# Two of four depthwise-convolution blocks moved from VectorE to ScalarE and GpSimd

## The chip, the cores and the metric

The kernel runs on one core of a Trainium2 chip. A core has a matrix engine (TensorE, PE in the rows), a vector engine (VectorE, DVE), an engine for activation functions (ScalarE, ACT), a general engine (GpSimd, POOL) and a queue that issues transfers (SyncE, SP). Each of them works through its own instructions in order, and they wait for each other on semaphores. On-chip data lies in SBUF (128 partitions); PE writes to PSUM.

The metric is the device time of one execution in microseconds (us), lower is better.

## The reference

A trunk of two layers on 512 tokens of 1024 channels, in float32. Each layer mixes tokens in three parallel branches, merges them with gates, and adds a feed-forward block and a gated per-layer input:

```python
proj = h @ w_in[i]
qa, ka, va, glu_in, qc, kc, vc, gates = jnp.split(proj, SPLITS, axis=-1)
ya = diff_attention(qa, ka, va, ...)
yb = conformer_conv(glu_in, conv_w[i], conv_b[i], cln_g[i], cln_b[i])
yc = neighbourhood_attention(qc, kc, vc, rpb[i])
ga, gb, gc = jnp.split(jax.nn.sigmoid(gates), 3, axis=-1)
merged = (ga * (ya @ w_br_a[i]) + gb * (yb @ w_br_b[i])
          + gc * (yc @ w_br_c[i]))
x = x + merged @ w_o[i]
```

The change is in the convolution of branch b: 512 channels, each with 31 taps of its own along the tokens, then a bias, a layer norm over the channels and a SiLU:

```python
a, g = jnp.split(u, 2, axis=-1)
z = a * jax.nn.sigmoid(g)
z = lax.conv_general_dilated(z, conv_w, window_strides=(1,), padding=[(15, 15)],
                             feature_group_count=CB, ...)
z = layernorm(z + conv_b, cln_g, cln_b)
return jax.nn.silu(z)
```

## The kernel before

Activations lie transposed: channels on the partitions, the 512 tokens along the free dimension, so that 512 channels are four blocks of 128x512. Every product with weights is made of three matmuls (`mm3`, L179): weights and activations are each split into a high part (a rounded copy, made by ScalarE) and a low part (the remainder, a subtraction on VectorE), both stored as float32r. `weights` (L170) loads a weight tile into a `wr` buffer, makes `wh` on ScalarE and `wl` on VectorE; there are three buffers of each, so the split of a tile waits until PE has done with the tile three before it. A tile is 128x1024 for a projection of the layer's input (24 matmuls of 512 columns, below called p), and 128x512 for a branch's output weights (12 matmuls, below called b).

PE's order is the order in which the code is written. The other engines' instructions are ordered by a scheduler from priorities (the place in the code, with pulls forward for weights) and from when it takes their inputs to be ready; on the chip each engine then keeps that order and waits where an input is late.

The order of a layer's phases: the gated input of the convolution (glu), neighbourhood attention (natten), differential attention (diff) with the gates of branch c (gatec) between, then branch c (`branch_c`, L786: one b tile for each of eight column blocks m), two of the gates of b (gateb, m = 2 and 3), merge a (`merge_a`, L793: for each of eight blocks a p tile for the gate and then a b tile), then `conv` (L566: sums the four convolution blocks, layer norm, SiLU), the remaining gates of b, merge b, the output projection, the feed-forward block.

The convolution itself is a list of VectorE instructions: for each of the four blocks j (`glu_z` tiles in, `conv_z` tiles out) one `tensor_scalar` with the bias and then 30 `scalar_tensor_tensor` (`c = src * w + c`), 124 in a layer. `taps` (L539) yields them one after another, and `background` (L554) takes a few at each of many places in the phases, as many as the table `BG` (L49) says, each placed behind a named instruction of its phase. By the sums of the table, 56 are issued up to the first two gates of b, and the rest in branch c, gates of b and merge a; `conv` issues what is left over.

The tiles that matter: `conv_z` and `glu_z` share five `z` buffers, so the third output block must wait until the taps of the second block have read their input; `rp` has four buffers, and is used by the query and key rotation of diff, by the split of the convolution's sum, and later in the output projection.

Of the kernel before, what the change touches and what calls it, by code (L numbers as in the profile page):

```python
# [14 lines left out]
AF = mybir.ActivationFunctionType  # L15
ALU = mybir.AluOpType
# [4 lines left out]
P = 128  # L21
# [3 lines left out]
GR = 8  # L25
# [5 lines left out]
CON3W = 31  # L31
# [15 lines left out]
PAR = L * PAR_L + 8  # L47
WARM = 8
BG = dict(glu=2, natten=1, values=3, diff=1, gatec=2, branchc=2, gateb=4, mergea=4, mergea2=2)  # L49
FIRST = (["v"] * 4 + ["pt"] * 2 + ["y", "b"], ["y"] * 5 + ["pt"] * 2 + ["b"])  # L50
EARLY = 6
QUARTERS = (2, 4, 6)
# [13 lines left out]
class Net:  # L66
# [229 lines left out]
    def build(self):  # L296
        nc, tc, a = self.nc, self.tc, self.a
        self.bufs = dict(wr=3, wh=3, wl=3, h=8, qk=2, kh=2, v=4, pt=2, y=5, z=5, x=4, t=7, rp=4,
                         e=4, a=3, r=2, rb=1, ss=1, sm=8, rc=4, b=2, s=8)
        self.bg, self.w_ahead = BG, 400  # L300
        self.pbufs = dict(mm=3, sc=2, tr=2, av=1)
# [12 lines left out]
    def opening(self):  # L314
# [23 lines left out]
        for k in range(KD):  # L338
# [6 lines left out]
            if k == 0:  # L345
                first = head[:, KD:]
                nc.vector.tensor_copy(hi[:, :P], first)
                self.tt(lo[:, :P], first, hi[:, :P].bitcast(F32), ALU.subtract)
            h.append(self.operand(xc[k], head[:, k:k + 1], FIRST[0][k]))
            c = slice(0 if k else P, 512)  # L350
# [81 lines left out]
    def layer(self, i, h, xsrc, xs):  # L432
        self.i, self.h = i, h
        zs, cs = [], []
        self.todo = self.taps(zs, cs)
        self.glu(zs)
        if i == 0:
            self.lambdas()
        yc, ya, yb = [], [], []
        sn, sd = {}, {}  # L440
        self.natten_in(0, sn, yc)
        self.drain(self.renorm)
        self.h = self.hs
        self.natten_v(sn)
        last = self.glu_last(zs)
        self.natten_in(1, sn, yc)
        next(last)
        self.natten_in(2, sn, yc)
        next(last)
        self.natten_in(3, sn, yc)  # L450
        acc, gb = [], []
        self.diff_in(0, sd, ya)
        self.diff_v(0, sd)
        self.diff_in(1, sd, ya)
        self.gate_c(acc, 0)
        self.diff_in(2, sd, ya)
        self.diff_v(1, sd)
        self.diff_in(3, sd, ya)
        for m in range(1, KD):
            self.gate_c(acc, m)  # L460
        for m in range(2):
            self.gate_b(gb, m, AF.Copy, None)
        for g in acc + gb:
            self.act(g, g, AF.Sigmoid, table="sigmoid")
        self.branch_c(acc, yc)
        for m in range(2, 4):
            self.gate_b(gb, m, AF.Sigmoid, "sigmoid")
        self.merge_a(ya, acc)
        conv = self.run(self.conv(cs, yb))
        pairs = self.inputs()  # L470
        for m in range(4, KD):
            self.gate_b(gb, m, AF.Sigmoid, "sigmoid")
            for n in ((0, 1), (2,), (3,), ())[m - 4]:
                self.input_block(pairs, n)
        self.drain(conv)
        mg = self.merge_b(yb, acc, gb)
        ws = self.pair_weights(4)
        x, h = self.w_o(mg, xsrc)
        self.input_pair(ws, pairs, 4)
        h = self.ffn(h, x)  # L480
        return self.ple(h, x, xs, self.inputs())
# [56 lines left out]

    def taps(self, zs, cs):  # L539

        for j, z in enumerate(zs):
            zf = z.rearrange("p a b -> p (a b)")
            c = self.sb("z", [P, 512])
            cs.append(c)
            for d in range(CON3W):
                w = self.par(self.i, "cw", j * CON3W + d)
                src = zf[:, d * GR:d * GR + 512]
                if d == 0:
                    yield self.nc.vector.tensor_scalar(c, src, w, self.par(self.i, "cb", j),
                                                       ALU.mult, ALU.add)  # L550
                else:
                    yield self.stt(c, src, w, c, ALU.mult, ALU.add)

    def background(self, after, n):  # L554

        ph, self.phase = self.phase, "conv"
        for _ in range(n):
            i = next(self.todo, None)
            if i is not None:
                self.tc.add_manual_dep(  # L560
                    i.ins, after.ins.name,
                    mybir.DependencyInfo(mybir.DependencyClass.NoSync, mybir.DependencyReason.DATA),
                    reason="background")
        self.phase = ph

    def conv(self, cs, ys):  # L566
        self.phase = "conv"
        nc, i = self.nc, self.i
        for _ in self.todo:
            pass  # L570
        sm = self.sb("ss", [P, 512])
        self.tt(sm, cs[0], cs[1], ALU.add)
        self.tt(sm, sm, cs[2], ALU.add)
        self.tt(sm, sm, cs[3], ALU.add)
        hi, lo = (self.sb("rp", [P, 512], F32R) for _ in range(2))
        self.split(hi, lo, sm)
        yield 2
        mu = self.ps("tr")
        nc.tensor.matmul(mu, self.ones_r, hi, start=True, stop=False)
        nc.tensor.matmul(mu, self.ones_r, lo, start=False, stop=True)  # L580
        st = []
        for j, c in enumerate(cs):
            self.stt(c, mu, -1.0 / CB, c, ALU.mult, ALU.add)
            self.sumsq(j, c, st)

        def done(col, rb):
            for j, c in enumerate(cs):
                self.tt(c, c, rb, ALU.mult)
                sg = self.sb("t", [P, 512])
                self.act(sg, c, AF.Sigmoid, table="sigmoid",  # L590
                         scale=self.par(i, "lg", j), bias=self.par(i, "lb", j))
                self.nc.vector.tensor_scalar(c, c, self.par(i, "lg", j), self.par(i, "lb", j),
                                             ALU.mult, ALU.add)
                if j % 2 == 0:
                    two = self.parts_of("qk", [2, 512], 2, F32R)
                y = two[j % 2]
                self.tt(c, c, sg, ALU.mult)
                self.split(y[:, 0, :], y[:, 1, :], c)
                ys.append(y)

        yield from self.norm(st[0], CB, (3, 1), done)
# [184 lines left out]
    def branch_c(self, acc, ys):  # L786
        self.phase = "branchc"
        for m in range(KD):
            ps = self.ps("mm")
            self.gemm(ps, self.a["w_br_c"][self.i, m], ys)  # L790
            self.background(self.tt(acc[m], acc[m], ps, ALU.mult), self.bg["branchc"])

    def merge_a(self, ys, acc):  # L793
        self.phase = "mergea"
        for m in range(KD):
            ps = self.proj(OFF_G + m * P)
            g = self.sb("t", [P, 512])
            self.background(self.act(g, ps, AF.Sigmoid, table="sigmoid"), self.bg["mergea"])
            pb = self.ps("mm")
            self.gemm(pb, self.a["w_br_a"][self.i, m], ys)  # L800
            self.tt(g, g, pb, ALU.mult)
            self.background(self.tt(acc[m], acc[m], g, ALU.add), self.bg["mergea2"])

    def gate_b(self, gs, m, func, table):
        self.phase = "gateb"
        ps = self.proj(OFF_G + D + m * P)
        if m % 2 == 0:
            gs += self.parts_of("v", [512], 2)
        self.background(self.act(gs[m], ps, func, table=table), self.bg["gateb"])

    def merge_b(self, ys, acc, gs):
        self.phase = "mergeb"
        out = []
        for m in range(KD):
            pb = self.ps("mm")
            self.gemm(pb, self.a["w_br_b"][self.i, m], ys)
            self.tt(gs[m], gs[m], pb, ALU.mult)
            self.tt(acc[m], acc[m], gs[m], ALU.add)
            mg = self.sb("y" if m < 5 else "v", [P, 2, 512], F32R)
            self.split(mg[:, 0, :], mg[:, 1, :], acc[m])  # L820
            out.append(mg)
        return out
# [366 lines left out]
    def ple(self, h, x, xs, pairs):  # L1189
# [4 lines left out]
        for m in range(KD - 2 * last):  # L1194
# [24 lines left out]
            def rest(m=m, pi=pi, g=g):  # L1219
# [6 lines left out]
                else:  # L1226
                    nc.sync.dma_start(xs[m], x[m])
                    hn.append(self.norm_chunk(m, x[m], self.par(i + 1, "mix", m), FIRST[1][m], st))

# [254 lines left out]
```

## Time and profile before

| what | value |
|---|---|
| median of the runs | 1769.13 us (1768.71 to 1769.55) |
| span of the profiled execution, first to last instruction | 1766.6 us |
| PE busy | 1759.3 us |
| DVE busy | 1408.6 us |
| ACT busy | 885.5 us |
| POOL busy | 98.4 us |

The profile is of one execution; its span is the time between its first and last instruction, and the median of the runs lies 2.5 us above that. Busy times are sums over instructions and overlap between engines. A row of the timeline gives the start and the duration in us, the engine, the line (L), the operation, out<-in by the program's names, the shape, a count, and in brackets how long the engine stood idle before and what ended that. A row of the groups gives the count, then busy us and mean ns of one, then the idle time before. A row of the waits gives who waited for whom, the sum in us, how often, and the longest. A row of the windows gives a stretch, its length, and each engine's busy time in it. The two layers are alike and lie 875 us apart; times are given for the first.

### The profile page before, as it was taken

What the parts mean: (1) busy time and instruction counts of PE and PEld (TensorE: products, weight loads), DVE (VectorE), ACT (ScalarE), POOL (GpSimd) and SP (SyncE); (2) the same over time, 40 slices, a digit from 0 to 9 for tenths busy, and PEclk for the clock granted to TensorE, in tenths of its full rate; (3) what the DMA queues carried; (4) which work ended last, traced back from release to release, by engine and by line L of the source; (5) the groups of instructions that cost most, each with busy time, mean ns of one, the idle gap of its engine ahead of it and who ended that gap; (6) DMA issues with size and microseconds to landing.
All of it is one profiled execution on the core that took longest, in us unless ns stands there. A gap on an engine that the chain in (4) does not pass through costs nothing.

```text
span 1766.6 us, 27127 instructions
## 1 busy us (share of the span) xinstructions
PE 1759.3 (100%) x10146; PEld 1551.8 (88%) x10146; DVE 1408.6 (80%) x2354; ACT 885.5 (50%) x1529; POOL 98.4 (6%) x114
## 2 busy tenths in 40 slices
PE   9999999999999999999999999999999999999998
PEld 7888888888899899998888888888888998989987
DVE  7967988998898587787777688889887976867776
ACT  5576555325565254454545655552356643534444
POOL 0000000000111010100000000000001110101000
PEclk9999999999999999999999999999999999999999
DMA  6575641334757365544446655322356674655332
GB/s 231 158 186 160 162 123 54 102 100 150 222 153 196 106 173 156 137 126 127 151 137 173 180 148 154 108 73 94 101 183 194 168 179 118 172 141 156 99 104 96
DMA packets 112548, 253.95 MB, mean 144 GB/s; under 512 B 14368, under 2 KB 23328, under 8 KB 112416
## 3 DMA queue, kind: packets, MB, share of 16 engines
q1 hardware_dynamic: 99024, 227.83, 42.0%
q0 software_dynamic: 12672, 23.07, 8.1%
q8 instruction: 80, 1.31, 0.3%
q10 hardware_dynamic: 720, 1.31, 0.2%
q14 instruction: 52, 0.43, 0.1%
HBM read 214.41 MB, written 7.34 MB: 126 GB/s over the span
## 4 chain that ended last, share of the span: by engine, by line
PE 92%; DVE 4%; DMA 2%; ACT 2%; issue 1%; SPq 0%; POOL 0%; ACTq 0%; POOLq 0%; DVEq 0%
PE ffn_mm L1034 4%; PE ffn_mm L1036 4%; PE ffn_mm L182 4%; PE ffn_mm L181 4%; PE ffn_mm L183 4%; PE ffn_mm L1035 4%; PE ffn_sc L1036 3%; PE ffn_sc L1034 3%; PE ffn_sc L1035 3%; PE mergea_mm L182 2%; PE mergea_mm L183 2%; PE mergea_mm L181 2%; PE gateb_mm L182 2%; PE gateb_mm L183 2%; PE gateb_mm L181 2%; PE wo_mm L182 2%
## 5 line engine op out<-in xcount | busy, mean ns | idle before, releaser
L164 DVE SCALAR_TENSOR_TENSOR conv_z<-glu_z,pre_par,conv_z 128x512 f32<-128x512 f32 x240 | 179.6, 748 | 3.5
L147 ACT ACTIVATE ffn_wh<-ffn_wr 128x1024 fp32r<-128x1024 f32 (+1 forms) x92 | 92.8, 1015 | 111.9 <-PE ffn_mm L182 81.4
L1004 POOL DMA_DIRECT2D ffn_qk<-w_fu x88 | 78.1, 978 | 605.6 <-DMA ffn_qk<-w_fu 289.7
L161 DVE TENSOR_TENSOR ffn_wl<-ffn_wr,ffn_wh 128x1024 fp32r<-128x1024 f32 (+1 forms) x92 | 107.4, 1173 | 5.3 <-ACT ffn_wh L147 4.6
L161 DVE TENSOR_TENSOR ffn_t<-ffn_mm,wo_rb 128x512 f32<-128x512 f32 (+1 forms) x64 | 38.7, 605 | 68.4 <-PE ffn_mm L183 68.4
L147 ACT ACTIVATE mergea_wh<-mergea_wr 128x1024 fp32r<-128x1024 f32 (+1 forms) x32 | 27.1, 848 | 96.8 <-PE mergea_mm L182 79.5
L147 ACT ACTIVATE ffn_wh<-ffn_qk 128x1024 fp32r<-128x1024 f32 x44 | 46.7, 1061 | 37.1 <-PE ffn_mm L182 15.9
L161 DVE TENSOR_TENSOR ffn_wl<-ffn_qk,ffn_wh 128x1024 fp32r<-128x1024 f32 x44 | 53.9, 1224 | 10.7 <-ACT ffn_wh L147 10.7
L161 DVE TENSOR_TENSOR ffn_t<-ffn_t,ffn_t 128x512 f32<-128x512 f32 (+1 forms) x46 | 31.3, 680 | 31.9 <-ACT ffn_t L147 31.4
L147 ACT ACTIVATE natten_e<-natten_e,natten_s 128x192 f32<-128x192 f32 (+1 forms) x88 | 39.3, 474 | 25.2 <-DVE natten_s L726 21.9
L181 PE MATMUL ffn_mm<-ffn_v,ffn_wh 128*128 128x512 f32 x132 | 51.4, 389 | 0.0
L182 PE MATMUL ffn_mm<-ffn_v,ffn_wh 128*128 128x512 f32 x132 | 51.4, 389 | 0.0
L183 PE MATMUL ffn_mm<-ffn_v,ffn_wl 128*128 128x512 f32 x132 | 51.3, 389 | 0.0
L181 PE MATMUL ffn_mm<-ffn_y,ffn_wh 128*128 128x512 f32 x132 | 51.3, 389 | 0.0
L182 PE MATMUL ffn_mm<-ffn_y,ffn_wh 128*128 128x512 f32 x132 | 51.3, 389 | 0.0
L183 PE MATMUL ffn_mm<-ffn_y,ffn_wl 128*128 128x512 f32 x132 | 51.3, 389 | 0.0
L147 ACT ACTIVATE diff_a<-diff_sc,diff_s 128x512 f32<-128x512 f32 x32 | 22.0, 687 | 57.1 <-DVE diff_s L919 57.0
L1036 PE MATMUL ffn_mm<-wo_h,ffn_wl 128*128 128x256 f32 x176 | 49.8, 283 | 0.0
L1036 PE MATMUL ffn_sc<-wo_h,ffn_wl 128*128 128x256 f32 x176 | 49.8, 283 | 0.0
L1035 PE MATMUL ffn_sc<-wo_h,ffn_wh 128*128 128x256 f32 x176 | 49.8, 283 | 0.0
L1035 PE MATMUL ffn_mm<-wo_h,ffn_wh 128*128 128x256 f32 x176 | 49.8, 283 | 0.0
L1034 PE MATMUL ffn_sc<-wo_h,ffn_wh 128*128 128x256 f32 x176 | 49.8, 283 | 0.0
(879 smaller groups left out, 6539.8 us busy)
## 6 DMA issues: line engine op xcount, KB each, us to landing
ffn_qk<-w_fu POOLq DMA_DIRECT2D x88, 256.0 KB, 5.7
ffn_wr<-w_fg SPq DMA_DIRECT2D x44, 512.0 KB, 3.7
ffn_wr<-w_fd SPq DMA_DIRECT2D x32, 448.0 KB, 4.1
ffn_r<-w_fu SPq DMA_DIRECT2D x44, 256.0 KB, 4.2
ffn_qk<-w_fg SPq DMA_DIRECT2D x44, 256.0 KB, 4.0
ffn_qk<-w_fu SPq DMA_DIRECT2D x44, 256.0 KB, 4.2
natten_wr<-w_in SPq DMA_DIRECT2D x16, 512.0 KB, 4.3
diff_wr<-w_in SPq DMA_DIRECT2D x16, 512.0 KB, 4.2
```

Of the source, the lines that this page charges most:

```text
L147: i = self.nc.scalar.activation(out, in_, func, **kw)
L161: return self.nc.vector.tensor_tensor(out, a, b, op)
L164: return self.nc.vector.scalar_tensor_tensor(out, a, s, b, op0, op1)
L181: mm(out, wh, ah, start=first, stop=False)
L182: mm(out, wh, al, start=False, stop=False)
L183: mm(out, wl, ah, start=False, stop=last)
L1004: nc.gpsimd.dma_start(q, wu[:, lo], accum_op=ALU.add)
L1034: mm(out, wh[:, c], bh, start=first and k == 0, stop=False, skip_group_check=True)
L1035: mm(out, wh[:, c], bl, start=False, stop=False, skip_group_check=True)
L1036: mm(out, wl[:, c], bh, start=False, stop=k == 3, skip_group_check=True)
```

## The change

Blocks 0 and 1 stay on VectorE as before (62 instructions in a layer). Blocks 2 and 3 are issued by a second generator, `spread_taps`: ScalarE makes a tap's product into an `rp` tile, GpSimd adds it to the block's accumulator; the first tap with the bias is one ScalarE instruction. A new table, `POOL`, says how many taps `share` takes at each place of branch c, gates of b and merge a: 8 x 2, 2 x 3, 8 x 2 and 8 x 2, so 54 of 62; `conv` issues the other eight.

```diff
+POOL = dict(branchc=2, gateb=3, mergea=2, mergea2=2)
@@ layer
-        self.todo = self.taps(zs, cs)
+        two = []
+        self.todo, self.more = self.taps(zs, cs), self.spread_taps(zs, two)
...
-        conv = self.run(self.conv(cs, yb))
+        conv = self.run(self.conv(cs, two, yb))
@@ taps
-        for j, z in enumerate(zs):
-            zf = z.rearrange("p a b -> p (a b)")
+        for j in range(2):
+            zf = zs[j].rearrange("p a b -> p (a b)")
...
+    def spread_taps(self, zs, cs):
+
+        for j in range(2, 4):
+            zf = zs[j].rearrange("p a b -> p (a b)")
+            c = self.sb("z", [P, 512])
+            cs.append(c)
+            for d in range(CON3W):
+                w = self.par(self.i, "cw", j * CON3W + d)
+                src = zf[:, d * GR:d * GR + 512]
+                if d == 0:
+                    self.act(c, src, AF.Identity, scale=w, bias=self.par(self.i, "cb", j))
+                else:
+                    t = self.sb("rp", [P, 512])
+                    self.act(t, src, AF.Copy, scale=w)
+                    self.nc.gpsimd.tensor_tensor(c, c, t, ALU.add)
+                yield
+
+    def share(self, name):
+
+        ph, self.phase = self.phase, "conv"
+        for _ in range(POOL[name]):
+            next(self.more, None)
+        self.phase = ph
@@ conv
-    def conv(self, cs, ys):
+    def conv(self, cs, two, ys):
...
-        for _ in self.todo:
-            pass
+        for todo in (self.todo, self.more):
+            for _ in todo:
+                pass
+        cs += two
@@ branch_c, merge_a, gate_b
             self.background(self.tt(acc[m], acc[m], ps, ALU.mult), self.bg["branchc"])
+            self.share("branchc")
...
             self.background(self.act(g, ps, AF.Sigmoid, table="sigmoid"), self.bg["mergea"])
+            self.share("mergea")
...
             self.background(self.tt(acc[m], acc[m], g, ALU.add), self.bg["mergea2"])
+            self.share("mergea2")
...
         self.background(self.act(gs[m], ps, func, table=table), self.bg["gateb"])
+        if m >= 2:
+            self.share("gateb")
```

PE's order is the same in both kernels. What the scheduler made of the change on ScalarE and VectorE is shown at the two places below; `mergea_wh` and `mergea_wl` are the high and low weight halves, `conv_rp` a tap's product, `conv_ss` the running sum of the convolution's blocks.

ScalarE in merge a of the first layer, from the b tile of block 3 to the b tile of block 4, before:

```order
L147 ACTIVATE mergea_wh_3605<-mergea_wr_3604 128x512
L147 ACTIVATE mergea_t_3536<-mergea_mm_3505 128x512
L147 ACTIVATE mergea_wh_3628<-mergea_wr_3627 128x1024
L147 ACTIVATE mergea_wh_3665<-mergea_wr_3664 128x512
L147 ACTIVATE mergea_t_3597<-mergea_mm_3566 128x512
```

The same piece now:

```order
L148 ACTIVATE mergea_wh_3669<-mergea_wr_3668 128x512
L148 ACTIVATE mergea_t_3594<-mergea_mm_3563 128x512
L148 ACTIVATE conv_rp_3961<-glu_z_836,pre_par_67 128x512
L148 ACTIVATE conv_rp_3964<-glu_z_836,pre_par_67 128x512
L148 ACTIVATE conv_rp_3967<-glu_z_836,pre_par_67 128x512
L148 ACTIVATE mergea_wh_3696<-mergea_wr_3695 128x1024
L148 ACTIVATE conv_rp_3970<-glu_z_836,pre_par_67 128x512
L148 ACTIVATE conv_rp_3973<-glu_z_836,pre_par_67 128x512
L148 ACTIVATE conv_rp_3976<-glu_z_836,pre_par_67 128x512
L148 ACTIVATE conv_rp_3979<-glu_z_836,pre_par_67 128x512
L148 ACTIVATE conv_rp_3986<-conv_ss_3982 128x512
L148 ACTIVATE mergea_wh_3735<-mergea_wr_3734 128x512
```

The last seven of the 60 products stand between these weights, and the split of the convolution's sum (`conv_rp<-conv_ss`), which came after merge a before, now stands ahead of block 4's b tile. In the blocks ahead of this piece it is the same picture: from the b tile of block 1 to that of block 3 each p tile has three products ahead of it, and each b tile seven.

VectorE at the same place, from the b tile of block 3 to the b tile of block 4, before:

```order
L161 TENSOR_TENSOR mergea_wl_3606<-mergea_wr_3604,mergea_wh_3605 128x512
L549 TENSOR_SCALAR conv_z_3539<-glu_z_836,pre_par_67 128x512
L161 TENSOR_TENSOR conv_ss_3862<-conv_ss_3862,conv_z_3212 128x512
L164 SCALAR_TENSOR_TENSOR conv_z_3539<-glu_z_836,pre_par_67,conv_z_3539 128x512
L161 TENSOR_TENSOR mergea_t_3536<-mergea_t_3536,mergea_mm_3543 128x512
L161 TENSOR_TENSOR mergea_wl_3629<-mergea_wr_3627,mergea_wh_3628 128x1024
L164 SCALAR_TENSOR_TENSOR conv_z_3539<-glu_z_836,pre_par_67,conv_z_3539 128x512
L161 TENSOR_TENSOR gatec_x_2594<-gatec_x_2594,mergea_t_3536 128x512
L164 SCALAR_TENSOR_TENSOR conv_z_3539<-glu_z_836,pre_par_67,conv_z_3539 128x512 x3
L161 TENSOR_TENSOR mergea_wl_3666<-mergea_wr_3664,mergea_wh_3665 128x512
```

The same piece now:

```order
L162 TENSOR_TENSOR mergea_wl_3670<-mergea_wr_3668,mergea_wh_3669 128x512
L162 TENSOR_TENSOR mergea_t_3594<-mergea_t_3594,mergea_mm_3601 128x512
L162 TENSOR_TENSOR gatec_x_2594<-gatec_x_2594,mergea_t_3594 128x512
L162 TENSOR_TENSOR mergea_wl_3697<-mergea_wr_3695,mergea_wh_3696 128x1024
L162 TENSOR_TENSOR conv_ss_3982<-conv_ss_3982,conv_z_3599 128x512
L162 TENSOR_TENSOR conv_rp_3987<-conv_ss_3982,conv_rp_3986 128x512
L162 TENSOR_TENSOR mergea_wl_3736<-mergea_wr_3734,mergea_wh_3735 128x512
```

The taps (`conv_z` by `scalar_tensor_tensor`) are gone from here. The addition of the last block to `conv_ss` and the low half of its split (`conv_rp`), which stood behind merge a's last blocks before, now stand between block 4's two weight tiles. The addition of the third block to `conv_ss` likewise stands earlier, ahead of block 1's b tile.

## The prediction, before the run

> **What bounds the kernel now.** I read the page's busy times first, then the waits of TensorE (PE), then the stage that the change touches as one stretch of the windows view.
>
> ```profile
> span 1766.6 us, 27127 instructions
> PE 1759.3 (100%) x10146; PEld 1551.8 (88%) x10146; DVE 1408.6 (80%) x2354; ACT 885.5 (50%) x1529; POOL 98.4 (6%) x114
> PE pre_av L329 <- DVE pre_zeror L402: 1.1, 1, 1.1
> PE natten_av L763 <- DVE natten_a L161: 0.3, 1, 0.3
> core 0: us, PE busy (x) PEld busy (x) DVE busy (x) ACT busy (x) POOL busy (x), PEclk, DMA share, GB/s
> 309.00:368.00 59.00, 59.00 (x264) 48.86 (x263) 55.01 (x76) 17.12 (x24) 0.00 (x0) 1.00 0.34 103
> ```
>
> PE is without work for 1766.6 - 1759.3 = 7.3 us of the whole span, and the waits that the trace names for it come to 1.4 us. In the first layer's stretch from late branch c to merge a's fifth column block, PE is busy for all 59 us. VectorE (DVE) is 93% busy there and still never late for PE; ScalarE (ACT) is idle for 42 us and GpSimd (POOL) for all 59. So VectorE time taken out here buys nothing by itself: at most the 7.3 us could be won anywhere, and any new wait of PE is added to the end one for one.
>
> **The change: what goes.** Each layer loses the 62 tap instructions of two channel blocks on DVE.
>
> ```profile
> L164 DVE SCALAR_TENSOR_TENSOR conv_z<-glu_z,pre_par,conv_z 128x512 f32<-128x512 f32 x41 | 30.7, 749 | 0.7
> ```
>
> That is about 62 x 0.75 = 46 us of DVE time per layer, counted at nothing, because PE beside it has no gap to close. The 60 taps per layer before this point stay where they were, as the order shows.
>
> **What comes: ScalarE.** 60 products and 2 first taps per layer. The nearest row is eight copies of the same shape run in a row.
>
> ```profile
> 289.27 4.29 ACT L147 ACTIVATE gatec_x<-gatec_x 128x512 f32<-128x512 f32 x8
> ```
>
> At 4.29/8 = 0.54 us each, 62 cost 33 us. With the 17.1 us of ACT work already in the 59 us stretch that is 50, so ACT alone has room. Four products are moved up into the diff stage, 2.2 us in all, between instructions that wait on DVE there; I count them at nothing, and at 2 x 2.2 = 4 us if that cover is not there.
>
> **What comes: GpSimd.** 60 additions per layer, 128x512, each waiting for the one before it (same accumulator) and for its product. The trace has no such addition. The nearest rows:
>
> ```profile
> L1473 POOL MEMSET const-float32-0.0<- 128x1 f32 x1 | 0.1, 99 | 0.2 <-issue 0.2
> masks.py:197 POOL MEMSET pre_ident<- 128x128 f32 x1 | 0.2, 205 | 0.3 <-POOLq L1473 0.3
> masks.py:199 POOL TENSOR_SCALAR_AFFINE_SELECT pre_ident<-pre_ident 128x128 f32<-128x128 f32 x1 | 0.3, 294 | 0.1
> 277.23 1.01 POOL L227 TENSOR_TENSOR diff_rc<-diff_sm,pre_power 128x4 f32<-128x4 f32 x1 [29.56 <-DVE diff_sm L164]
> L1297 POOL TENSOR_TENSOR ple_rc<-ple_sm,pre_power 128x1 f32<-128x1 f32 x4 | 2.3, 574 | 43.5 <-DVE ple_sm L164 43.5
> ```
>
> Writing costs (205 - 99)/127 = 0.83 ns a column; reading and writing (the select) (294 - 99)/127 = 1.54, so reading 0.70. Two reads and a write make 2.24 ns, times 512 is 1.14, plus the 0.10 start: **1.24 us**, which I take. Below, an addition that costs no more than a write: 0.10 + 512 x 0.83 ns = 0.53. Above, a start as the power operation shows it: from 0.57 for one column and 1.01 for four, 0.147 a column, so 0.43 before the first column, hence 0.43 + 1.14 = 1.57.
>
> The Trainium skill (GPSIMD Engine Reference, 3.1) gives 4497 ns for such an addition of 2048 columns; a quarter is 1.12 us, an estimate by that page, which would take 2 x 60 x 0.12 = 14 us off the sum below. No run here shows it.
>
> **Do the two engines get in each other's way?** Of the power operations on POOL above (1.01 us), one is longer in each layer, and it is the one that starts while DVE runs a tap, which reads two SBUF tensors.
>
> ```profile
> 277.00 0.68 DVE L919 TENSOR_REDUCE diff_s<-diff_sc 128x1 f32<-128x512 f32 x1
> 307.53 1.43 POOL L227 TENSOR_TENSOR diff_rc<-diff_sm,pre_power 128x4 f32<-128x4 f32 x1 [29.30 <-PE branchc_mm L182]
> 307.35 0.75 DVE L164 SCALAR_TENSOR_TENSOR conv_z<-glu_z,pre_par,conv_z 128x512 f32<-128x512 f32 x1
> 1182.54 1.44 POOL L227 TENSOR_TENSOR diff_rc<-diff_sm,pre_power 128x4 f32<-128x4 f32 x1 [29.27 <-PE branchc_mm L182]
> ```
>
> 1.43 - 1.01 = 0.42: POOL stood until 307.95, which is 0.60 after the tap's start. The one of 277.23, beside the reduction out of PSUM, lost nothing. So each DVE instruction with two SBUF inputs seems to take about 0.60 us of POOL per 512 columns.
>
> The Trainium skill (SBUF — State Buffer, Who interferes with whom) says this outright: such a DVE instruction and a GpSimd one that reads SBUF exclude each other, the later one waits for the whole earlier one. It speaks against this change, which puts the moved work on the one engine that shares its port with the relieved one. By it, the sum holds the lock term that follows; without it that term is zero. The trace agrees, with the 0.42.
>
> While the additions run, the order leaves DVE these instructions with two SBUF inputs: 13 of 512 columns (four low weight halves of merge a and one of branch c, three of the diff outputs, three additions into the accumulators, two of the convolution's sum) and 7 of 1024 (five weight halves of merge a, two of gate b).
>
> ```profile
> L161 DVE TENSOR_TENSOR mergea_wl<-mergea_wr,mergea_wh 128x1024 fp32r<-128x1024 f32 x6 | 7.3, 1224 | 1.0 <-ACT mergea_wh L147 0.6
> L161 DVE TENSOR_TENSOR mergea_wl<-mergea_wr,mergea_wh 128x512 fp32r<-128x512 f32 x5 | 3.5, 693 | 1.6 <-ACT mergea_wh L147 1.6
> 314.88 1.22 DVE L161 TENSOR_TENSOR gateb_wl<-gateb_wr,gateb_wh 128x1024 fp32r<-128x1024 f32 x1
> 316.01 0.74 DVE L164 SCALAR_TENSOR_TENSOR conv_z<-glu_z,pre_par,conv_z 128x512 f32<-128x512 f32 x1
> ```
>
> 13 x 0.60 + 7 x 1.1 (starts 1.13 apart) = **15.5 us** of POOL per layer. Ends: 0 and 15.5.
>
> **The wait that it adds.** Products live in four `rp` buffers, so product k waits for addition k - 4, and ACT runs in order. Behind these products on ACT stand the high halves of merge a's weights; behind the convolution's two sums on DVE (moved up ahead of the weights of blocks 1 and 4) stand the low halves; PE waits for both. The last such place is block 4's 512-column weight (b4): in the new order it stands behind the 60th addition, the last sum and its split.
>
> ```profile
> 307.47 0.63 ACT L147 ACTIVATE branchc_wh<-branchc_wr 128x512 fp32r<-128x512 f32 x1 [2.58 <-PE branchc_mm L182]
> 359.62 0.64 ACT L147 ACTIVATE mergea_wh<-mergea_wr 128x512 fp32r<-128x512 f32 x1 [4.38 <-PE mergea_mm L182]
> 360.29 0.69 DVE L161 TENSOR_TENSOR mergea_wl<-mergea_wr,mergea_wh 128x512 fp32r<-128x512 f32 x1 [0.28 <-ACT mergea_wh L147]
> 367.81 0.39 PE L181 MATMUL mergea_mm<-diff_y,mergea_wh 128*128 128x512 f32 x1
> ```
>
> The first tap follows the weight of 307.47 on ACT, and POOL is free at 307.53 + 1.43 = 309.0. The chain ends at 309.0 + 60 x 1.24 + 15.5 = 398.9. Then sum on DVE (0.7), split on ACT (0.6), b4's high half (0.6), its low half (0.7) and four handovers of about 0.05 (360.26 to 360.29 is one): 2.8. PE gets b4 at 401.7, and wanted it at 367.8: **33.9 us late**. In earlier tiles it is late by less, since the additions need more time per block than PE, 10 x 1.24 against 8.16 us (the 367.81 less four blocks is 335.2); the lateness is one number that grows, not a sum of tiles. After b4, ACT is free and the weights run ahead of PE again. Nothing later gives time back, as PE has no gaps there. Two layers: 67.8.
>
> Sum: 1766.6 + 67.8 = 1834.4 in the span; the median before, 1769.13, lies 2.5 above the span: **1837 us**.
>
> **The rivals.**
> 1. *The port does not cost, or the adds are cheaper.* The 0.42 us was seen on a tiny operation, and gaps between additions may hold the DVE work. Without the lock term: 18.4 late per layer, 1769.1 + 36.8 = 1806; with the 0.10 start hidden behind the addition before as well, 60 x 1.14 gives 12.4, so 1794. Against it: both layers show the longer power operation alike, 1.43 and 1.44. Band 1788 to 1815.
> 2. *The start of an addition is 0.43, not 0.10.* 309.0 + 60 x 1.57 + 15.5 + 2.8 - 367.8 = 53.7 late per layer, 1769.1 + 107.4 = 1877. For it: the only two-input rows on POOL have that start; against it, the power is not an addition, and may spend it on its own work. Band 1859 to 1890.
> 3. *Not slower: the additions keep up.* The price that decides is (367.8 - 2.8 - 309.0)/60 = 0.93 us for an addition, lock included. At 0.53 and the whole lock term the chain ends at 356.3, ACT carries 50 of its 59 us, and the time stays at 1769. Against it: the select, one read cheaper than an addition, already costs 0.10 + 512 x 1.54 ns = 0.89. Faster would need more than the 7.3 us that PE is idle.
> 4. *The clock falls in PE's new pauses.* At the start, matmuls of this shape took 3.78/8 = 0.47 us; later their starts are 0.23 apart.
>
> ```profile
> 1.06 3.78 PE L329 MATMUL pre_av<-pre_zeror 128*128 128x512 f32 x8 [1.06 <-DVE pre_zeror L402]
> 367.58 0.39 PE L183 MATMUL mergea_mm<-glu_h,mergea_wl 128*128 128x512 f32 x1
> ```
>
> PE would pause some 5 us before each 512-column weight (seven additions and their lock share, 10.4, less the 5.4 of the 24 matmuls before). Slow matmuls in between hide behind POOL; only b4's twelve would count, 12 x 0.24 = 2.9 per layer, 1843. The Trainium skill (TensorE: Matmul & The Clock Gate, Part 1) puts the fall at about 3.4 us of idle time; no pause of the trace tests it.
>
> **How the numbers follow.** Forecast, 1816 to 1858: 0.48, half of it with rival 4, which stays inside that band. Rival 1: 0.21; rival 2: 0.18; rival 3, up to 1788: 0.11; faster: 0.02. A measurement of this kernel tells about 2% from no change, here 35 us, or 1804.5. That puts rival 3 and a third of rival 1 into "same": 0.18; slower 0.80; faster 0.02. The range 1792 to 1880 leaves out rival 3, faster, and the outer ends of 1 and 2, some 0.19 in all.
>
> **What would show it.** Right: PE busy time as before, with new waits of PE on `mergea_wh`/`mergea_wl` of some 34 us in each layer; ACT products waiting for `conv_z` on POOL; POOL busy by 150 us or more above 98.4; DVE `mergea_wl` longer or late where an addition runs; DVE down by about 90 us; the stretches outside branch c to merge a unchanged. Wrong: additions under 0.93 us from start to start, PE gapless in merge a, or PE waits in the diff stage (the moved products) or in the convolution's end.

## The result, and the profile after

The changed kernel takes **1842.65 us** (1842.1 to 1843.2) against 1769.13 before: a ratio of 1.0416, 95% interval 1.0386 to 1.0446. Predicted were 1837, from 1792 to 1880. The profiled execution has a span of 1840.3 us, 73.7 more than the one before, or 36.9 per layer.

The page's span and busy times, after:

```profile
span 1840.3 us, 27360 instructions
...
PE 1789.4 (97%) x10146; PEld 1565.3 (85%) x10146; DVE 1349.5 (73%) x2230; ACT 967.4 (53%) x1653; POOL 273.7 (15%) x234
```

PE is now without work for 1840.3 - 1789.4 = 50.9 us, 43.6 more than before, or 21.8 per layer; and its busy time itself grew by 30.1 us, with the same 10146 matmuls. Together that is the 73.7. DVE fell by 59.1, not by the 93 that 124 taps of 0.75 us are.

The waits of PE (in all, times, longest), after, the five largest; the others are 5.2 us together, 3.8 of them in gate b:

```profile
PE mergea_mm L182 <- ACT mergea_t L148: 13.2, 7, 3.4
PE mergea_mm L184 <- DVE mergea_wl L162: 11.2, 8, 2.3
PE mergea_mm L182 <- ACT gateb_v L148: 6.7, 2, 4.1
PE mergea_mm L182 <- ACT mergea_wh L148: 5.5, 4, 1.8
PE mergea_mm L182 <- DVE gatec_x L162: 2.9, 2, 2.3
```

The engines named, ACT and DVE, were themselves held up, as the groups of instructions show (busy, mean ns, idle before and what ended it):

```profile
L570 POOL TENSOR_TENSOR conv_z<-conv_z,conv_rp 128x512 f32<-128x512 f32 x120 | 175.3, 1461 | 9.2
...
L148 ACT ACTIVATE conv_rp<-glu_z,pre_par 128x512 f32<-128x512 f32 x120 | 86.0, 721 | 69.0 <-POOL conv_z L570 68.9
...
L162 DVE TENSOR_TENSOR mergea_wl<-mergea_wr,mergea_wh 128x1024 fp32r<-128x1024 f32 (+1 forms) x32 | 41.8, 1312 | 79.1 <-ACT mergea_wh L148 79.1
```

ACT stood for 68.9 us ahead of its products, each time until an addition on POOL was done; DVE stood for 79.1 us ahead of the low weight halves, until ACT had made the high ones. The chain is POOL, ACT, DVE, PE.

Layer 0's chain on POOL, ACT and DVE behind it, and PE's block 4 (b4), from the timeline of after:

```profile
308.87 92.16 POOL L570 TENSOR_TENSOR conv_z<-conv_z,conv_rp 128x512 f32<-128x512 f32 x60
...
401.07 0.69 DVE L162 TENSOR_TENSOR conv_ss<-conv_ss,conv_z 128x512 f32<-128x512 f32 x1 [7.97 <-POOL conv_z L570]
...
401.79 0.63 ACT L148 ACTIVATE conv_rp<-conv_ss 128x512 fp32r<-128x512 f32 x1 [5.43 <-DVE conv_ss L162]
402.33 0.61 ACT L148 ACTIVATE mergea_wh<-mergea_wr 128x512 fp32r<-128x512 f32 x1
...
403.48 0.50 PE L182 MATMUL mergea_mm<-diff_y,mergea_wh 128*128 128x512 f32 x1 [3.42 <-ACT mergea_t L148]
...
404.67 0.63 PE L183 MATMUL mergea_mm<-diff_y,mergea_wh 128*128 128x512 f32 x1
...
407.94 0.40 PE L182 MATMUL mergea_mm<-glu_h,mergea_wh 128*128 128x512 f32 x1
```

The additions run without a gap from 308.87 to 401.03; then come sum, split, b4's high half and PE, as predicted, link by link. PE starts b4 at 403.48 where it was 367.81, and the block after it at 407.94: 12 matmuls in 4.46 us, at starts of up to 0.43 us apart instead of 0.23.

Windows of the stretch with the chain and of one far from it (us, then busy time and instructions of PE, PEld, DVE, ACT, POOL, then PEclk, DMA share, GB/s):

```profile
309.00:405.00 96.00, 74.05 (x267) 55.83 (x266) 39.30 (x35) 56.30 (x83) 87.49 (x60) 0.87 0.18 56
450.00:900.00 450.00, 450.00 (x2869) 410.67 (x2868) 353.65 (x564) 223.15 (x341) 41.35 (x46) 1.00 0.55 153
```

Of these 96 us PE has work for 74, at a clock of 0.87; far from them it has work all the time, as before.

### The profile page after: what moved, and what is told of

Same layout as the page of the kernel before. It is cut to its first block, busy times and chain, and to the rows that moved or that the text cites. A ratio compares the mean times of both kernels' runs of the same rounds, so it can differ in the third digit from the quotient of the medians.

```text
span 1840.3 us, 27360 instructions
## 1 busy us (share of the span) xinstructions
PE 1789.4 (97%) x10146; PEld 1565.3 (85%) x10146; DVE 1349.5 (73%) x2230; ACT 967.4 (53%) x1653; POOL 273.7 (15%) x234
## 4 chain that ended last, share of the span: by engine, by line
PE 82%; POOL 9%; DVE 3%; ACT 2%; issue 1%; DMA 1%; SPq 0%; POOLq 0%; ACTq 0%; DVEq 0%
POOL conv_z L570 9%; PE ffn_mm L1067 4%; PE ffn_mm L1069 4%; PE ffn_mm L183 4%; PE ffn_mm L184 4%; PE ffn_mm L182 4%; PE ffn_mm L1068 4%; PE ffn_sc L1069 3%; PE ffn_sc L1067 3%; PE ffn_sc L1068 3%; PE wo_mm L182 2%; PE wo_mm L183 2%; PE wo_mm L184 2%; PE diff_sc L861 1%; PE gatec_mm L183 1%; PE gatec_mm L182 1%
## 5 line engine op out<-in xcount | busy, mean ns | idle before, releaser
L570 POOL TENSOR_TENSOR conv_z<-conv_z,conv_rp 128x512 f32<-128x512 f32 x120 | 175.3, 1461 | 9.2
L148 ACT ACTIVATE conv_rp<-glu_z,pre_par 128x512 f32<-128x512 f32 x120 | 86.0, 721 | 69.0 <-POOL conv_z L570 68.9
L162 DVE TENSOR_TENSOR mergea_wl<-mergea_wr,mergea_wh 128x1024 fp32r<-128x1024 f32 (+1 forms) x32 | 41.8, 1312 | 79.1 <-ACT mergea_wh L148 79.1
L228 POOL TENSOR_TENSOR diff_rc<-diff_sm,pre_power 128x4 f32<-128x4 f32 x8 | 8.9, 1116 | 563.7 <-DVE diff_sm L165 505.2
L165 DVE SCALAR_TENSOR_TENSOR conv_z<-glu_z,pre_par,conv_z 128x512 f32<-128x512 f32 x120 | 89.7, 747 | 1.3
L1068 PE MATMUL ffn_sc<-wo_h,ffn_wh 128*128 128x256 f32 x176 | 49.8, 283 | 0.0
```

What stands on the lines that cost most here:

```text
L148: i = self.nc.scalar.activation(out, in_, func, **kw)
L162: return self.nc.vector.tensor_tensor(out, a, b, op)
L165: return self.nc.vector.scalar_tensor_tensor(out, a, s, b, op0, op1)
L570: self.nc.gpsimd.tensor_tensor(c, c, t, ALU.add)
L1068: mm(out, wh[:, c], bl, start=False, stop=False, skip_group_check=True)
```

## The experiments

The theory: the chain of 60 additions per layer, at its price from start to start and with what it loses to DVE, paces ACT's products in their order, and merge a's weights stand behind them. The lateness is the chain's end against the moment at which PE wants b4. Rivals: the load and order of ACT's new work; contention of DVE and GpSimd as the main part; the place of the convolution's sum on DVE.

### The size of an addition

```diff
-                    self.nc.gpsimd.tensor_tensor(c, c, t, ALU.add)
+                    self.nc.gpsimd.tensor_tensor(c[:, :256], c[:, :256], t[:, :256], ALU.add)
```

> Each of the 60 additions per layer takes 256 of the 512 columns (the other half of each sum is left out); products, orders and waits stay. Theory, the chain of additions sets the end: an addition then costs about 0.75 us from start to start instead of 1.36, the chain ends at 309 + 60 x 0.75 + 10.5 of contention = 364.5 instead of 401.0, block 4's weights reach PE at about 367, when PE wants them (367.8): 1769 to 1775 us. Rival A, ACT's own load and the new order of its work are what makes merge a late: nothing of that changes, 1825 to 1845. Rival B, contention with VectorE is the main part and the size of an addition matters little: 1800 to 1825.

Measured: **1775.74 us**, 1.0040 (1.0025 to 1.0055). The additions in this run's tile view (durations in ns, min/median/max, then first and last start), the same row of the changed kernel, and the chain in this run's timeline:

```profile
L570 POOL TENSOR_TENSOR conv_z<-conv_z,conv_rp x120: 730/742/1614, 309.8 to 1246.7; 128x256 f32<-128x256 f32 x120
```

```profile
L570 POOL TENSOR_TENSOR conv_z<-conv_z,conv_rp x120: 1264/1292/2158, 308.9 to 1312.7; 128x512 f32<-128x512 f32 x120
```

```profile
309.80 59.76 POOL L570 TENSOR_TENSOR conv_z<-conv_z,conv_rp 128x256 f32<-128x256 f32 x60
```

The chain ends at 369.56, not at the 364.5 expected, since a half addition costs 0.82 and not 0.75 us from start to start. By the prediction's tail of 2.8, b4 is then at 372.4, less the 0.8 by which this chain began later 371.6, 3.8 behind 367.8: 7.6 in two layers; 6.6 were measured. All of ACT's products, the order of work and the number of meetings are still there, so rivals A and B fall: what costs the time is the length of the chain.

The two sizes also give the price by parts: (1.292 - 0.742)/256 = 2.15 ns a column, and 0.19 us for the start. The chain view of after shows what lies between two additions (start, us, what):

```profile
327.69 1.63 POOL conv_z L570
329.31 0.04 issue
329.35 0.02 POOLq L570
329.37 0.02 issue
329.39 1.62 POOL conv_z L570
...
332.78 2.14 POOL conv_z L570
...
335.00 1.30 POOL conv_z L570
```

0.08 us of handover, so 1.29 + 0.08 = 1.37 for an addition that meets nothing; 0.33 more where it met a DVE instruction of 512 columns, 0.85 where it met one of 1024.

### The place of the sum

```diff
-        self.tt(sm, sm, cs[2], ALU.add)
-        self.tt(sm, sm, cs[3], ALU.add)
+        for c in cs[2:]:
+            self.behind(self.tt(sm, sm, c, ALU.add), self.last)
```

`self.last` is merge a's last addition into an accumulator; `behind` orders without a semaphore.

> Only the two additions of the convolution's sum that need the new blocks are moved, on VectorE, behind merge a's last addition; the products stay where they are, ahead of block 4's weight. Theory: block 4's high half then waits only for product 60, so for addition 56 (395.6 instead of 401.0 and the sum's 1.5): 5 to 7 us less per layer, 1829 to 1833. Rival A, the sum on VectorE is the whole cause: 1769 to 1780. Rival B, the products ahead of the weight alone decide and the sum adds nothing: 1841 to 1844.

Measured: **1832.46 us**, 1.0358 (1.0343 to 1.0374), so 5.1 less per layer. The last product on ACT and b4's high half, which starts at once behind it (402.33 in the changed kernel):

```profile
396.22 0.72 ACT L148 ACTIVATE conv_rp<-glu_z,pre_par 128x512 f32<-128x512 f32 x1 [0.64 <-POOL conv_z L570]
396.85 0.61 ACT L148 ACTIVATE mergea_wh<-mergea_wr 128x512 fp32r<-128x512 f32 x1
```

The weight now waits for addition 56 instead of the 60th and its sum. The sum's place is worth that and no more: the products ahead of the weight are the bulk.

### Fewer meetings with DVE

```diff
+            if self.phase == "mergea":
+                self.low = self.act(hi[:, :n], raw[:, :n], AF.Copy)
+                return hi, hi
             self.low = self.split(hi[:, :n], lo[:, :n], raw[:, :n])
```

> The changed kernel without the low halves of merge a's weights (their VectorE subtraction is left out; TensorE multiplies by the high half in their place, so its work is the same). That takes 4 instructions of 512 and 5 of 1024 columns with two SBUF inputs from beside the chain, and the low half behind block 4's high half. Theory, each costs the chain what it was seen to cost (0.34 and 0.86 us): 5.7 + 0.7 = 6.4 us less per layer, 1830, from 1826 to 1833. By the prediction's 0.60 and 1.1 us: 8.6 less, 1825. Rival, the gaps between additions hold the VectorE work and the price of an addition is all: only the 0.7 go, 1841.

Measured: **1833.9 us**, 1.0367 (1.0352 to 1.0383), just above the theory's 1826 to 1833. The chain, from the timeline:

```profile
311.27 86.30 POOL L573 TENSOR_TENSOR conv_z<-conv_z,conv_rp 128x512 f32<-128x512 f32 x60
```

92.16 - 86.30 = 5.86 us shorter, where 5.7 was expected of the contention seen; the prediction's 0.60 and 1.1 would have made it 7.9. The time fell by 8.7 us and not by 12.8, for two reasons that the trace shows. In layer 0 the chain begins 2.4 us later than in the changed kernel, behind a wait of PE of 1.4 us at 159 us that the changed kernel does not have; what the wait and the rest of the 2.4 come from stays open. And PE's pauses ahead of b4 are longer, 5.84 and 5.80 us, so that b4's matmuls are slow in both layers: 4.19 and 4.72 us, where the changed kernel has 4.46 and 2.86, so 1.6 us more in sum.

### One block of four

```diff
-        for j in range(2):
+        for j in range(3):
...
-        for j in range(2, 4):
+        for j in range(3, 4):
```

> Only one channel block goes to ScalarE and GpSimd, three stay on VectorE. Theory: 30 additions per layer; the last product stands ahead of block 1's weight and waits for addition 26. With VectorE doing 31 more taps of two SBUF inputs, nearly every addition meets one (+0.34 us): addition 26 ends at 309 + 26 x 1.7 = 353, block 1's weights are there at 355, PE wants them at 367.8 - 3 x 8.16 = 343.3: 12 us late per layer, 1793; without those meetings 3 us late, 1776. So 1776 to 1793. Rival, every moved addition costs its share (half of the 73 us): 1806.

Measured: **1799.29 us**, 1.0173 (1.0156 to 1.0190): outside the theory's 1776 to 1793, and below the rival's 1806. From its timeline the chain on POOL, and DVE up to block 1's low half:

```profile
308.64 47.11 POOL L570 TENSOR_TENSOR conv_z<-conv_z,conv_rp 128x512 f32<-128x512 f32 x30
...
350.33 0.86 DVE L551 TENSOR_SCALAR conv_z<-glu_z,pre_par 128x512 f32<-128x512 f32 x1 [1.93 <-ACT conv_rp L148]
351.23 5.06 DVE L165 SCALAR_TENSOR_TENSOR conv_z<-glu_z,pre_par,conv_z 128x512 f32<-128x512 f32 x3
356.22 0.68 DVE L162 TENSOR_TENSOR mergea_wl<-mergea_wr,mergea_wh 128x512 fp32r<-128x512 f32 x1
```

The chain was somewhat faster than expected, 1.57 us per addition instead of 1.7, and block 1's high half was there at 350.82 instead of some 355; the working missed DVE. Its third block could not begin before 350.33: the trace names a product as what it waited for, and it starts right behind the last of the 30. That fits the five `z` buffers, since the last product is also the last to read block 3's input; no run tests it. Then three taps beside additions took 5.06 us (2.3 alone) ahead of block 1's low half, which was there at 356.90, 13.6 late by the 343.3 of the expectation. So the wait behind the chain is there as the theory has it, with a term on DVE that it had left out; the equal share per addition (1806) lies outside the interval, which ends at 1803.

### The same work at PE's pace

```diff
-POOL = dict(branchc=2, gateb=3, mergea=2, mergea2=2)
+POOL = dict(branchc=2, gateb=3, mergea=3, mergea2=2)
...
-            next(self.more, None)
+            i = next(self.more, None)
+            if i is not None:
+                self.behind(i, after)
```

`after` is the instruction of merge a (or branch c, gate b) beside which the product is written.

> The same work in the same places of the program, but each product is tied behind the instruction beside which it was written, so that the scheduler cannot draw the products together ahead of block 4: five products per block of merge a, all eight blocks. Theory, the chain's pace against PE's: 5 x 1.53 us (1.36 and its share of the contention) = 7.65 us per block against PE's 8.16, so GpSimd keeps up and ends with merge a at about 400: 1769 to 1780. Rival A, the additions cost 92 us of waiting wherever they stand: 1830 to 1850. Rival B, VectorE and GpSimd contend and PE waits for the low weight halves of each block by some 1 to 2 us: 1785 to 1805.

Measured: **1793.53 us**, 1.0139 (1.0123 to 1.0154): 49 us less than the changed kernel with the same instructions, but not the 1769 to 1780; it lies in rival B's 1785 to 1805. The chain in its timeline, and the two largest waits of PE:

```profile
309.78 99.93 POOL L570 TENSOR_TENSOR conv_z<-conv_z,conv_rp 128x512 f32<-128x512 f32 x60
```

```profile
PE conv_tr L609 <- ACT conv_rp L148: 12.4, 2, 6.3
PE mergea_mm L184 <- DVE mergea_wl L162: 3.4, 4, 0.9
```

Rival A falls: PE goes through merge a almost without a wait. But spread over all of merge a, the additions meet more of DVE's work: 99.93/60 = 1.67 us each instead of 1.53, so 5 x 1.67 = 8.3 per block, just above PE's 8.16; the chain ends at 409.71, and the convolution's sum behind it makes PE wait 6.2 us in each layer. The size that failed is the contention. Rival B's number is met, but not by its mechanism: PE's waits for the low halves of merge a are 3.4 us in all, and not 1 to 2 us in each block. Most of the 24 us are the two waits of 6.2 us and slower matmuls: PE's busy time is 1767.6 us, 8.3 above that of the kernel before.

The test of the pace alone is the same kernel with half additions, as in the first experiment:

> Products tied to their places, five per block of merge a, and each addition takes 256 of the 512 columns (the other half of each sum is left out). Theory, only the pace of the additions against PE's block counts: 5 x 1.0 to 1.15 us (1.0 with the contention of the half additions untied) is 5.0 to 5.8 us against 8.16, so the chain ends with merge a and nothing waits: 1769 to 1773. Rival A, ScalarE's 33 us of products or their order cost by themselves: 1778 to 1795. Rival B, VectorE is late because of the meetings whatever the pace: 1775 to 1790.

Measured: **1770.15 us**, 1.0004 (0.9994 to 1.0013): the time before. The group of its additions, and the window with the chain:

```profile
L570 POOL TENSOR_TENSOR conv_z<-conv_z,conv_rp 128x256 f32<-128x256 f32 x120 | 110.0, 917 | 69.9 <-ACT conv_rp L148 63.3
```

```profile
309.00:405.00 96.00, 95.77 (x425) 78.96 (x424) 52.88 (x59) 63.80 (x101) 55.17 (x61) 1.00 0.31 99
```

Now POOL waits for ACT (63.3 us) and not ACT for POOL; PE is busy for 95.77 of 96 us at full clock. Products, their order and the meetings of these half additions with DVE cost nothing once an addition's price is below the pace. And with DVE at 52.88 of 96 us instead of 86.64, the time is not below the time before: DVE's relief is worth nothing here.

The third of this kind, one block at three additions per block of merge a:

```diff
-POOL = dict(branchc=2, gateb=3, mergea=3, mergea2=2)
+POOL = dict(branchc=1, gateb=1, mergea=1, mergea2=2)
```

with the two ranges of the one block above.

> One channel block on ScalarE and GpSimd, three on VectorE, each product tied behind the instruction beside which it was written, three per block of merge a. Theory: 3 x 1.67 us = 5.0 us of GpSimd per block against PE's 8.16, so ScalarE and PE never wait for an addition; VectorE gives 23 us per layer away and gets some 30 meetings of 0.8 us back, which is as much: 1769 to 1780. Rival A, every addition that waits on GpSimd costs its share, as in the one block without ties: 1793 to 1803. Rival B, VectorE, 93% busy before, is late because of the meetings: 1780 to 1793. Faster than 1760 would speak against all three.

Measured: **1815.28 us**, 1.0263 (1.0248 to 1.0278), outside all of it. PE's only large wait, and DVE's timeline where it comes from:

```profile
PE conv_tr L609 <- ACT conv_rp L148: 41.2, 2, 20.6
```

```profile
391.11 1.52 DVE L551 TENSOR_SCALAR conv_z<-glu_z,pre_par 128x512 f32<-128x512 f32 x1
...
406.36 14.13 DVE L165 SCALAR_TENSOR_TENSOR conv_z<-glu_z,pre_par,conv_z 128x512 f32<-128x512 f32 x18
```

In merge a nothing waited, as expected of the pace. But DVE's third block began only with the last product, at 391, as in the one block without ties, and its 31 taps ended the convolution some 20 us late. Slowing the chain's products moved the moment at which that block may begin. What one block would cost without this wait, the run does not tell.

### The contention by itself

Three kernels, all with the work of the kernel before and a scratch tile added: with 48 additions per layer, with 124 fills, and with nothing on GpSimd.

```diff
+            self.idle = self.sb("idle", [P, 480], bufs=1)
+            self.nc.vector.memset(self.idle, 0.0)
...
+            self.behind(self.nc.gpsimd.tensor_tensor(self.idle, self.idle, self.idle, ALU.add), after)
```

> The kernel before, with nothing moved: all taps stay on VectorE, and GpSimd adds a scratch tile of 480 columns to itself 48 times per layer from the same moment on (309 us), which no engine waits for. Only contention can cost time. Theory, an addition and a VectorE instruction with two SBUF inputs exclude each other: in the runs so far the VectorE one then took about 0.8 us longer; 48 meetings are 38 us per layer, VectorE has about 7 us to spare in those 90 us, so PE is some 31 us late per layer: 1831, and from 1810 to 1840. Rival, contention costs GpSimd time and VectorE hardly any: 1769 to 1775.

Measured: **1823.61 us**, 1.0304 (1.0287 to 1.0321).

> The kernel before with nothing moved; GpSimd only writes: 124 fills of the same scratch tile of 480 columns per layer, some 0.5 us each by the fill rows of the trace (0.10 + 480 x 0.83 ns), about 62 us from 309 us on, which no engine waits for. Theory, it is GpSimd's reading that excludes a VectorE instruction with two SBUF inputs: 1769 to 1773. Rival A, any use of SBUF by GpSimd does it: 62 us of it as in the 48 additions, 1805 to 1830. Rival B, each meeting costs VectorE the rest of one fill, half of 0.5 us: 1775 to 1800.

Measured: **1783.01 us**, 1.0075 (1.0060 to 1.0090), with no wait of PE at the fills: above the theory's 1773 and inside rival B's range. The next run tells which it is.

> The kernel before with the scratch tile of 480 columns allocated (and set once) and nothing that uses it: the base of the two runs with GpSimd work that nobody waits for. In both of them the matmuls of some stages, those on natten_y, diff_y, conv_qk, mergeb_y, ffn_v and ffn_y, took 0.394 to 0.396 us where they take 0.389 to 0.391, also far from the place where GpSimd works. Theory, the scratch tile moves the tiles behind it in SBUF, and that alone costs this: 1780 to 1784, so the fills cost nothing and the additions some 41 us. Rival, GpSimd's work is the cause in some way: 1769 to 1771.

Measured: **1782.99 us**, 1.0078 (1.0061 to 1.0095). So the tile itself costs 13 us (see the last section), the fills cost nothing and rival B falls, and the additions 1823.61 - 1782.99 = 40.6 us, 20.3 per layer, though no engine waits for them. The additions of layer 0 in the timeline, and DVE in the stretch of 309 to 375 us, by form, with the additions; then the same rows of DVE in the kernel before:

```profile
311.14 69.08 POOL L559 TENSOR_TENSOR glu_idle<-glu_idle 128x480 f32<-128x480 f32 x48
```

```profile
L164 DVE SCALAR_TENSOR_TENSOR conv_z<-glu_z,pre_par,conv_z 128x512 f32<-128x512 f32 x29 | 38.3, 1320 | 0.5
...
L161 DVE TENSOR_TENSOR diff_y<-diff_t,diff_y 128x512 fp32r<-128x512 f32 x3 | 4.3, 1470 | 0.0
...
L161 DVE TENSOR_TENSOR gatec_x<-gatec_x,branchc_mm 128x512 f32<-128x512 f32 x5 | 3.4, 676 | 0.0
```

```profile
L164 DVE SCALAR_TENSOR_TENSOR conv_z<-glu_z,pre_par,conv_z 128x512 f32<-128x512 f32 x46 | 34.5, 749 | 0.8
...
L161 DVE TENSOR_TENSOR gatec_x<-gatec_x,branchc_mm 128x512 f32<-128x512 f32 x5 | 3.4, 683 | 0.0
...
L161 DVE TENSOR_TENSOR diff_y<-diff_t,diff_y 128x512 fp32r<-128x512 f32 x3 | 1.9, 684 | 0.0
```

What reads two SBUF tensors on DVE takes about twice its time (1320 for 749, 1470 for 684 ns), what reads one operand from PSUM (`branchc_mm`) none more. In the whole span DVE's busy time is 1464.5 against 1408.6: 0.58 us for each of the 96 additions. The theory's 31 us per layer was half too high, since not each addition finds something to meet; the rival is out. Of the 1823.61, 13 us are the tile's: the additions alone would make it 1769.1 + 40.6 = 1809.7, the lower end of the theory's 1810 to 1840.

## Why the prediction was right

The forecast rested on one mechanism, and the runs bear it out: it holds with b4's place (the sum moved), with the chain's length (half additions: 6.6 us left of 73.5) and with the pace (half additions in their places: nothing left). Its terms, for layer 0:

| step of the prediction | predicted | measured |
|---|---|---|
| DVE's relief is worth | nothing | nothing (1770.15 with DVE relieved and PE not held up) |
| chain starts at | 309.0 | 308.87 |
| an addition from start to start | 1.24 | 1.37 |
| the lock, GpSimd's side | 15.5 | 92.16 - 60 x 1.37 = 10.0 |
| chain ends at | 398.9 | 401.03 |
| from there to PE | 2.8 | 2.45 |
| PE gets b4 at | 401.7 | 403.48 |
| late per layer | 33.9 | 35.7, and 37.4 behind b4's matmuls |

Two terms were mis-sized and nearly cancel, which is luck. **The addition**: its columns were right (2.24 ns predicted, 2.15 measured), its start was not (0.10 taken, 0.19 and 0.08 of handover measured); rival 2's 0.43 was too much. That is 60 x 0.13 = 7.8 us too little. The Trainium skill (GPSIMD Engine Reference, 3.1) gives 4497 ns for 2048 columns. The estimate by its quarter, 1.12 us, was further off than 1.24 (1.29 measured), since the measured start does not shrink with the columns. **The lock**: 0.60 and 1.1 us per meeting were taken, 0.33 and 0.85 is what an addition lost: 5.5 us too much. The Trainium skill (SBUF — State Buffer, Who interferes with whom) has the later instruction wait for the whole earlier one. The traces agree that the two hold each other up, and show less than that: an addition lost only half of the DVE instruction's 0.69 us, and with the additions that nobody waits for, a DVE instruction took 1.47 us and one addition followed the other after 69.08/48 = 1.44, where one behind the other would be 0.68 + 1.22 = 1.90 (1.22 for 480 columns is an estimate from the two sizes above).

**Rival 4**, which was inside the band, came true in part: the clock fell around PE's pauses, PE's busy time grew by 30.1 us, and "PE busy time as before" was wrong, as were "new waits of some 34 us in each layer" (21.8, the rest is slower matmuls). Most of the slow matmuls lie under the waiting; only b4's 12 count. In layer 0 they took 4.46 us for the 2.72 (367.81 to 370.53 before). In layer 1 they ran at full clock, from here to 1319.32, 2.86 us:

```profile
1316.46 0.50 PE L182 MATMUL mergea_mm<-diff_y,mergea_wh 128*128 128x512 f32 x1 [2.17 <-ACT mergea_t L148]
```

So the clock cost 1.7 us in layer 0 and 0.1 in layer 1, where 2.9 per layer had been worked out. Of the 5.9 us by which the span grew beyond the 67.8 of the sum, these are 1.9; the others are b4's start, late by 35.7 in layer 0 and 36.2 in layer 1 (1316.46 against 1242.83 before, less the 37.4 of layer 0) instead of 33.9. That rival 4's 1843 is the time measured is therefore luck as well.

**Rival 1** (no lock) falls with the extra 40.6 us of additions that nobody waits for, and with the chain that is 5.86 us shorter without the low halves. **Rival 3** (the additions keep up) needs 0.93 us for one, contention included; half additions untied cost 0.996 and are 3.3 us late per layer, where that bound gives 60 x (0.996 - 0.93) = 4.0.

Wrong in the list of what would show it: DVE down by about 90 us (59.1). The working priced the lock for GpSimd alone; DVE gave 34 of the 93 us back in longer instructions. In the changed kernel DVE stood idle for 79.1 us ahead of merge a's low halves, which left room for it, and PE's 11.2 us of waits for them lie ahead of b4, whose start the chain sets. What kept the paced additions from restoring the time in full is GpSimd's side of the same contention, 1.67 us for an addition. The four products moved into the diff stage, counted at nothing, cost nothing: the chain starts at 308.87, and PE has no new wait ahead of gate b.

None of the versions beats the kernel before, and PE's 7.3 us without work leave little to win.

## What to carry to other kernels

Before work is moved to a free engine, compare its price per step there, handover included, with the pace of the engine that sets the end, and look for what stands in order behind the feeding instructions: here 1.37 us per addition against 0.93 allowed, and the weights of the matmuls behind the products. An addition on GpSimd beside a VectorE full of instructions with two SBUF inputs takes 0.58 us of VectorE away for the 0.75 that a tap had cost there, so the relief is mostly a loan; in the changed kernel, whose VectorE had less to do beside the additions, it was 34 us for 120 additions, 0.28 each. An engine that is 93% busy and never waited for is not a reason for a change; the relieved VectorE bought 0 us.

## What was not expected of the hardware

**An unused tile costs matmul time.** A scratch tile of 480 columns (1920 bytes per partition), set once and used by nobody, makes the kernel before 13 us slower (1782.99). PE has no new wait above 0.5 us; the matmuls of some stages take longer, all through the program. First the kernel before, then the one with the tile:

```profile
L182 PE MATMUL ffn_mm<-ffn_y,ffn_wh x132: 389/389/389, 575.8 to 1707.7; 128*128 128x512 f32 x132
```

```profile
L182 PE MATMUL ffn_mm<-ffn_y,ffn_wh x132: 390/393/396, 580.7 to 1722.6; 128*128 128x512 f32 x132
```

That the cause is the address of the tiles behind it is argued from this, not shown: no run moved a tile alone.

**The clock does not go by the length of one pause.** In the changed kernel matmuls start 0.43 us apart, instead of 0.23, for some 3.3 us after the 3.42 us ahead of b4. They do so too after a pause of 1.37 us in gate b and one of 2.24 us in merge a, but not after one of 2.67 us. The slow stretches of the first layer begin at 322.42, 346.31, 359.97, 377.03, 394.10 and 404.34 us, which are whole multiples of 3.41 us apart, and each lasts 3.41 us or twice that. So it is read in fixed windows of 3.41 us: the one that holds the whole pause of 2.24 us and the next, then the two between which the pause of 2.67 us (368.39 to 371.06) is divided:

```profile
356.55:359.96 3.41, 1.20 (x5) 1.02 (x6) 3.38 (x4) 2.43 (x4) 3.23 (x3) 1.00 0.06 11
359.96:363.37 3.41, 3.41 (x9) 2.62 (x9) 2.67 (x2) 1.38 (x2) 3.33 (x2) 0.50 0.38 143
...
366.79:370.20 3.41, 1.60 (x8) 0.98 (x6) 0.00 (x0) 2.13 (x4) 3.25 (x3) 1.00 0.00 0
370.20:373.61 3.41, 2.55 (x11) 2.13 (x12) 2.37 (x3) 2.15 (x4) 3.25 (x3) 1.00 0.36 91
```

In the first pair PE was idle for 3.41 - 1.20 = 2.21 us of a window, and the next ran at half the clock; in the second it was idle for 1.81 and 0.86 us, and the clock stayed. In the kernel without low halves the pause of 2.95 us was divided in the same way, 1.30 and 1.65 us, and the clock stayed too. Where the bound lies is not settled: in the changed kernel windows at full clock with 2.2 us of idle time or more were always followed by the slow clock, those with 1.4 or less never, and between 1.5 and 1.8 both happened. The Trainium skill (TensorE: Matmul & The Clock Gate, Part 1) puts both the idle time and the warm-up at about 3.4 us. The trace agrees on the length of a slow stretch; the clock fell after less idle time than that, and the measurement decides.

**GpSimd's writing costs VectorE nothing.** 62 us of fills per layer left DVE's taps at 749 ns. The Trainium skill (SBUF — State Buffer, Who interferes with whom) says so of an engine that only writes.
